# A Fourier input projection on folded operands, moved among the gate units, and an earlier start of the attention scan

## The chip, the cores and the metric

The kernel runs on one core of one Trainium2 chip. The metric is the device time of one execution in microseconds (us). Three runs of the kernel before took 1936.08, 1936.16 and 1936.3 us; the median is 1936.16 us. A profile of one execution on the chip is at hand, with every instruction's start and duration.

## The reference, cut to what matters

One layer of a diffusion backbone on T = 384 positions (128 context, 256 latent) by 2048 channels. The change touches the mixing sub-layer:

```
proj = h @ w_in                     # q 512 | k 512 | v 1024 | g 1024 | lr 32 | fo 1024
o = GLA(q, k, v, decay(lr)); o = rmsnorm(o) * silu(g)            # 4 heads, both directions
fg = fo.reshape(t, 4, 256)
f = fft2(fg, axes=(positions, channels of a group), norm='ortho').real
gates = sigmoid(h @ w_gate + b_gate)
merged = g_a * (o @ w_br_gla) + g_b * (f @ w_br_four)
m = merged @ w_out
```

Context and latent positions are transformed apart (lengths 128 and 256). All adaLN factors are linear maps of a condition, `silu(cond) @ w_ada`, with six blocks of 2048 columns.

## The kernel before, in words

Activations lie transposed, channels on the 128 partitions and the 384 positions along the row; weights come as blocks of 128x1024 f32 (512 KB). The products are f32 in three passes of fp32r: ScalarE (ACT) rounds a weight block to `whi` (L223), VectorE (DVE) forms the rest `wlo = raw - whi` (L224), and TensorE (PE) multiplies `whi` by both parts of the activations and `wlo` by the high one. One "unit" (`proj`) is one block of 128 output columns: two weight blocks ("halves"), each 8 x 3 matmuls of 384 columns.

A list `srcs` fixes the order in which blocks are loaded, and the code consumes them in the same order. `grab` (before each half) takes the next split block and pushes one more: it issues a load into one of two `raw` buffers and splits the block into one of four pairs of `whi`/`wlo` buffers. Three split blocks are ahead of PE at best. PE, ACT, DVE and GpSimd (POOL) run in the order that the code writes; only the DMA queue of SyncE (SP) is ordered by the scheduler.

Beside the products runs side work, handed out by generators: after each half the code calls `next` on them. `ada_rest` computes three of the adaLN blocks on DVE, in six halves of 16 steps (one 512 KB load, two instructions over 128x1024 each, L574), an empty step, a step with 16 small matmuls on the sums (`pr`, L582), and two transposes (`ptm`, L591) at the start of the next half. `paced` throttles it: with `rate` r it advances r steps for each call. It must have ended before the buffer of its sums is reused near the end of `w_out`, so the code empties it after unit 12 of `w_out`.

The stages, with their start in the profile:

- Head (0 us): norm, first adaLN blocks, `h` block by block (`hf`, 16 blocks, kept as `scr`), v and the first two q units (L488 to L529).
- 146 us: the two other q units, the decay factors (`plr`, L812, and the constants `a2`, L814 to L824), four k units; `ada` at rate 1.
- 197 us: 32 gate units (L841), each result stored to DRAM; beside them `ada` at rate 1 and `gla`, the scan of the four heads, in 61 steps.
- 501 us: eight Fourier input units. Two of them make the two half blocks of one group; DVE forms their sum and difference (L952, L953). Then a DFT over channels (`px`, L895, L896) and over positions (`pp`, L881) in plain f32; the result is kept on half of the frequencies only, as `eT` and `dT`.
- 590 us: the mixing stage. Eight units for g ("o", with `gcol`, L982 to L985), 16 Fourier branch blocks ("b", `four`, L998 to L1012, whose weights DVE folds first, L204 and L205) and 16 GLA branch blocks ("a", L1033, L1034) in an order written by hand; `ada` at rate 0.
- 758 us: 16 units of `w_out`, `ada` at rate 0.7. From 893 us: norms and the FFN.

Of the kernel before, what the change touches and what calls it, by code (L numbers as in the profile page):

```python
# [21 lines left out]
P = 128  # L22
# [16 lines left out]
XU = 2  # L39
# [10 lines left out]
HT = HC + HL  # L50
C_CR = C_SEL3 + 96
C_CT = C_CR + 129 + 129 + 128
C_LT = C_CT + 2 * HC
NC = C_LT + 2 * 2 * HL


def _constants():
# [25 lines left out]
    c[:, C_CR : C_CR + 129] = ce  # L83
    c[0, C_CR + 129 : C_CR + 258] = jj[0] % 2
    c[:, C_CR + 258 : C_CR + 386] = cs
    for base, n in ((C_CT, TC), (C_LT, TL)):
        h = n // 2 + 1
        ang = 2 * np.pi * (np.outer(np.arange(n), np.arange(h)) % n) / n
        sc = 1.0 / math.sqrt(n * GD)
        kk = n // P  # L90
        w = kk * h
        for k, m in enumerate((np.cos(ang) * sc, np.sin(ang) * sc)):
            c[:, base + k * w : base + (k + 1) * w] = m.reshape(kk, P, h).transpose(1, 0, 2).reshape(P, w)
# [4 lines left out]
def tile_step(ctx: ExitStack, tc: tile.TileContext, a, o):  # L98
# [48 lines left out]
    for i in range(XU, 8):  # L147
        srcs += two(a["w_in"], i)
    for i in range(32):
        srcs += two(a["w_gate"], i)  # L150
    for i in range(16, 24):
        srcs += two(a["w_in"], i)

    mix_order, n_b = [], 0
    for i in range(8):
        k = (0, 1, 1, 2, 1, 2, 1, 2)[i]
        mix_order += [("o", i)] + [("b", n_b + j) for j in range(k)]
        n_b += k
# [5 lines left out]
    folded = set()  # L164
    for b, i in mix_order:
        if b == "o":
            srcs += two(a["w_in"], 8 + i)
        elif b == "b":
            folded.add(len(srcs))
            srcs.append(a["w_br_four"][i])  # L170
        else:
            srcs.append(a["w_br_gla"][i])
# [17 lines left out]
    def load(raw=None):  # L190
        n, src = next(srcs, (0, None))
        if src is not None:
            if raw is None:
                raw = wp.tile([P, G], F32, tag="raw", name="raw", bufs=2)
            SP.dma_start(raw, src)
            raws.append((raw, n in folded))

    fold_in = []
# [11 lines left out]
    def split(at=None, eng=DVE, hold=False, defer=None):  # L210


        if raws:
            raw, pairs = raws.pop(0)
# [97 lines left out]

    hT = alloc_A()
    psm = ctx.enter_context(tc.tile_pool(name="psm", bufs=3, space=PSUM))
    pss = ctx.enter_context(tc.tile_pool(name="pss", bufs=5, space=PSUM))
    with ExitStack() as s:
# [47 lines left out]
        def load_later():  # L364
# [4 lines left out]
            SP.dma_start(selr, a["consts"][:, C_SELR : C_SELR + 64])  # L369

# [89 lines left out]
        for kb in range(KT):  # L460
# [74 lines left out]
            for sub in lag:  # L535
                sub()
            if kb:
# [8 lines left out]
        push()  # L546
        vr = [actp.tile([P, 3, 1024], F32R, tag=t, name="vr") for t in ("B_hi", "B_lo")]
# [65 lines left out]
    ada = paced(ada_gen, rate)  # L613
    with ExitStack() as s:
# [23 lines left out]
        def gla():  # L638
# [10 lines left out]
            for h in range(NH):  # L649
# [12 lines left out]
                yield  # L662
# [90 lines left out]
                yield  # L753
# [46 lines left out]
            for t in range(3):  # L800
                for h in range(NH):
                    z = on(t, h)
                    DVE.tensor_scalar_mul(z, z, rs[:, t, h : h + 1])
                yield
# [4 lines left out]
        for i in range(XU, 4):  # L809
            proj(psm, hT, keep(qT, i), ada)  # L810
# [14 lines left out]
        for i in range(4):  # L825
            proj(psm, hT, keep(kT, i), ada)

# [10 lines left out]
        for i in range(32):  # L838
            def gate(p, i=i):
                g = pg.tile([P, T], F32, tag="gz", name="gz", bufs=2)  # L840
                ACT.activation(g, p, AF.Identity, bias=bgate[:, i : i + 1])  # L841
                SP.dma_start(gates_d[i], g)

            proj(psm, hT, gate, sd)
# [5 lines left out]
    with ExitStack() as s:  # L850
        pc = s.enter_context(tc.tile_pool(name="pc", bufs=1))
        fold_in.append(pc)
        b0 = C_CR
        pw = 448
        d2 = pc.tile([P, 2 * pw], F32R, name="d2")
        cd = pc.tile([P, NC - b0], F32, name="cd")
        SP.dma_start(cd, a["consts"][:, b0:NC])
        oT = alloc_r("B", "o")


# [5 lines left out]
        nyq = pc.tile([P, 3, P], F32, name="nyq")  # L866
        POOL.memset(nyq, 0.0)


        wn = pc.tile([P, D], F32R, name="wn")  # L870
        done = [0]

        def dft():


            def left(dst, stat, m):

                for lat, base, n in ((0, C_CT - b0, HC), (1, C_LT - b0, HL)):
                    for k in range(1 + lat):
                        c0 = base + (m * (1 + lat) + k) * n  # L880
                        PE.matmul(  # L881
# [1141 lines left out]
```

## Time and profile before

| | |
|---|---|
| median of 3 runs | 1936.16 us (1936.08 to 1936.3) |
| span of the profiled execution, first to last instruction | 1934.3 us |
| PE busy | 1918.5 us (99%) |
| DVE busy | 1641.8 us (85%) |
| ACT busy | 1069.3 us (55%) |
| DMA moved | 429.12 MB, 222 GB/s |

The profiled execution has no time of its own beside its span; the median lies 1.9 us above that span, which is what lies ahead of the first instruction and behind the last one. "PEld" is a weight load of PE, "pmm" the accumulator of a unit. In a row of the chain of waits stand the start, the duration and the work that the time was spent on. In a row of the windows, "x" is a count of instructions. A matmul with two f32 operands shows as two records ("x2").

### The profile page before, as it was taken

To read this page: it belongs to the slowest core of one execution; us is meant where nothing else is said; L and a number is where in the kernel's file an instruction comes from. 1 tells how busy PE (TensorE), PEld (TensorE's weight loads), DVE (VectorE), ACT (ScalarE), POOL (GpSimd) and SP (SyncE) were. 2 spreads that over 40 slices of the span, in tenths; PEclk is the share of its full clock that TensorE was granted. 3 is DMA by queue.
4 is the path that set the end of the run, shared out by engine and by line. 5 is a ranking of instruction groups with operands and counts; after the bars stand their busy time and mean duration, and the time that the engine had idled before them with its cause. 6 is when DMAs were issued, how large, how long until landed. Compare 5 with 4: busy or idle time off the path is not lost.

```text
span 1934.3 us, 27954 instructions
## 1 busy us (share of the span) xinstructions
PE 1918.5 (99%) x10398; PEld 1702.5 (88%) x10398; DVE 1641.8 (85%) x2059; ACT 1069.3 (55%) x1523; POOL 145.2 (8%) x171
## 2 busy tenths in 40 slices
PE   8999999999999999999999999999999999999998
PEld 5779999999999999999988888888888888888886
DVE  5569888879776797977789999999999999988885
ACT  4233454554335655446556666766666666666555
POOL 0000000000000000002100111111111120211001
PEclk9999999999999999999999999999999999999999
DMA  9978676767754687654639696979788797969553
GB/s 389 371 263 269 228 257 219 241 219 259 256 190 145 204 287 246 218 185 154 231 98 280 155 284 151 262 170 244 191 243 207 212 230 192 252 136 253 158 199 128
DMA packets 246152, 429.12 MB, mean 222 GB/s; under 512 B 45308, under 2 KB 149948, under 8 KB 241664
## 3 DMA queue, kind: packets, MB, share of 16 engines
q1 hardware_dynamic: 199072, 386.70, 60.0%
q0 software_dynamic: 18432, 33.56, 11.3%
q10 hardware_dynamic: 28512, 7.08, 2.3%
q8 instruction: 81, 1.33, 0.3%
q14 instruction: 55, 0.45, 0.1%
HBM read 365.68 MB, written 54.53 MB: 217 GB/s over the span
## 4 chain that ended last, share of the span: by engine, by line
PE 97%; DMA 1%; DVE 1%; ACT 0%; issue 0%; SPq 0%; POOL 0%; DVEq 0%; POOLq 0%; ACTq 0%
PE pmm L257 36%; PE pgu L1539 31%; PE pdn L1539 10%; PE pds L1539 7%; PE pv L399 3%; PE pgm L382 1%; PE pf L998 1%; DMA slab<-in_w_ada 1%; PE px L417 1%; PE pmm L1253 1%; PE pf L999 1%; PE bk L1539 1%; PE po L647 1%; PE pr L582 0%; PE dl L647 0%; PE pp L881 0%
## 5 line engine op out<-in xcount | busy, mean ns | idle before, releaser
L257 PE MATMUL pmm<-A_hi,whi 128*128 128x384 f32 x1200 | 404.3, 337 | 0.0
L257 PE MATMUL pmm<-A_hi,wlo 128*128 128x384 f32 x1200 | 401.4, 334 | 0.0
L257 PE MATMUL pmm<-A_lo,whi 128*128 128x384 f32 x1200 | 401.3, 334 | 0.0
L1437 ACT CAST whi<-u 128x1024 fp32r<-128x1024 f32 x200 | 210.1, 1053 | 173.1 <-PE pds L1539 42.6
L223 ACT CAST whi<-raw 128x1024 fp32r<-128x1024 f32 x181 | 189.8, 1051 | 171.3 <-DMA raw<-in_w_gate 62.2
L1448 DVE TENSOR_TENSOR wlo<-u,whi 128x1024 fp32r<-128x1024 f32 x200 | 243.7, 1220 | 34.1 <-ACT whi L1437 32.5
L224 DVE TENSOR_TENSOR wlo<-raw,whi 128x1024 fp32r<-128x1024 f32 x179 | 217.9, 1220 | 52.5 <-ACT whi L223 49.7
L1539 PE MATMUL pgu<-whi,A_hi 128*128 128x512 f32 x640 | 249.9, 390 | 0.0
L1539 PE MATMUL pgu<-whi,A_lo 128*128 128x512 f32 x640 | 249.2, 389 | 0.0
L257 PEld LDWEIGHTS pmm<-A_hi,whi 128*128 128x128 f32 x1200 | 225.3, 188 | 2.9 <-issue 1.8
L257 PEld LDWEIGHTS pmm<-A_lo,whi 128*128 128x128 f32 x1200 | 225.4, 188 | 0.2
L257 PEld LDWEIGHTS pmm<-A_hi,wlo 128*128 128x128 f32 x1200 | 225.3, 188 | 0.0
L574 DVE SCALAR_TENSOR_TENSOR adacc<-adaw,cond,adacc 128x1024 f32<-128x1024 f32 x180 | 222.7, 1278 | 2.8 <-DMA adaw<-in_w_ada 2.5
L1437 ACT CAST whi<-raw 128x1024 fp32r<-128x1024 f32 x157 | 165.0, 1053 | 87.2 <-PE pgu L1539 27.9
L1448 DVE TENSOR_TENSOR wlo<-raw,whi 128x1024 fp32r<-128x1024 f32 x157 | 191.1, 1218 | 12.6 <-ACT whi L1437 12.2
L1539 PE MATMUL pgu<-wlo,A_hi 128*128 128x512 f32 x640 | 185.8, 389 | 0.0
L1539 PEld LDWEIGHTS pgu<-whi,A_hi 128*128 128x128 f32 x640 | 120.1, 188 | 25.9 <-issue 0.8
L1539 PEld LDWEIGHTS pgu<-wlo,A_hi 128*128 128x128 f32 x640 | 120.1, 188 | 25.1
L1539 PEld LDWEIGHTS pgu<-whi,A_lo 128*128 128x128 f32 x640 | 120.1, 188 | 24.7
L1539 PE MATMUL pgu<-whi,S 128*128 128x512 f32 x400 | 116.6, 389 | 0.0
L1672 POOL DMA_DIRECT2D sums_d<-spare x64 | 58.5, 950 | 625.3 <-ACT spare L1668 618.9
L1539 PE MATMUL pdn<-whi,hid_hi 128*128 128x512 f32 x264 | 102.8, 389 | 0.0
(410 smaller groups left out, 3302.3 us busy)
## 6 DMA issues: line engine op xcount, KB each, us to landing
adaw<-in_w_ada SPq DMA_DIRECT2D x96, 512.0 KB, 4.2
raw<-in_w_d SPq DMA_DIRECT2D x70, 512.0 KB, 5.2
slab<-in_w_ada SPq DMA_DIRECT2D x32, 1024.0 KB
raw<-in_w_gate SPq DMA_DIRECT2D x64, 512.0 KB, 4.5
raw<-in_w_g SPq DMA_DIRECT2D x48, 512.0 KB, 3.7
raw<-in_w_u SPq DMA_DIRECT2D x48, 512.0 KB, 5.2
raw<-in_w_in SPq DMA_DIRECT2D x44, 512.0 KB, 4.3
u<-in_w_u SPq DMA_DIRECT2D x40, 512.0 KB, 7.1
```

Source lines behind the costliest of these rows:

```text
L223: ACT.copy(hi, raw)
L224: sub = lambda: eng.tensor_sub(lo, raw, hi.bitcast(F32))
L257: PE.matmul(dst, w[wi][:, k * n + n0 : k * n + n0 + P], x[xi][:, k0 + k, :], start=first and k == 0 and j == 0, stop=last and k == kts - 1 ...
L382: PE.matmul(pgv[q : q + 32, :], spad[:, k, :], slab[k // (KT // 2)][:, k % (KT // 2), :], start=k < 4, stop=k >= KT - 4,)
L399: PE.matmul(pv[2 * t + g], hT[x_][:, kb, t * P : (t + 1) * P], w_[:, g * 512 : (g + 1) * 512], start=kb == 0 and j == 0, stop=kb == KT - 1 ...
L417: PE.matmul(px, w_[:, u * P : (u + 1) * P], hT[x_][:, kb, :], start=j == 0, stop=j == 2)
L574: DVE.scalar_tensor_tensor(acc[:, c, :], w, cond[:, k, c : c + 1], acc[:, c, :], op0=ALU.mult, op1=ALU.add,)
L647: PE.matmul(dst, w[wi], x[xi], start=first and j == 0, stop=last and j == 2)
L1437: ACT.copy(hi, src)
L1448: DVE.tensor_sub(lo, src, hi.bitcast(F32))
L1539: PE.matmul(dst, stat[x_][m], mov(w[w_], m), start=first and w_ == m == x_ == 0, stop=last and w_ == m == 1, skip_group_check=any(more),)
L1672: POOL.dma_start(sums_d[k], u, accum_op=ALU.add)
```

## The change

- In the head, `fold_h` makes sums and differences of mirrored positions of each block of `hf` (DVE), in the place of the spent input, and `keep_h` stores them to DRAM, 1.5 MB in each of two transfers. 194 columns of sums (65 context, 129 latent) and 190 of differences stand for the 384 positions.
- The Fourier input is taken out of the 8 units. The two weight blocks of a group are added and subtracted on DVE (kinds `p0`, `p1`), and the sums are multiplied by the position sums alone, the differences by the position differences alone. The first columns of a pair of blocks (channels 0 and 128 of a group) have no mirror image; their difference on the position sums is added from `bn`, a small product with these columns, which are loaded by themselves (`wnr`, elements of 4 bytes).
- The eight groups' halves are done among the last 8 of the 32 gate units, the folded `h` is read back and split during the two gate units ahead of them, and the DFTs work on the folded positions.
- The k units come first and the scan starts after the first of them, with two steps fewer in each head; the last scaling moves to ACT.
- `ada` runs at rate 1 until gate unit 22, at 0.5 for two units, at 1 to unit 32, at 0.75 in the "o" units of the mixing stage; `w_out` stays at 0.7. Two o units go ahead of the first b.

```diff
+    QK = (4, 5, 6, 7, 2, 3)
+    GF, FO0 = 22, 24
...
     for i in range(32):
         srcs += two(a["w_gate"], i)
+        if i >= FO0:
+            g, kh = divmod(i - FO0, 2)
+            for n in range(2):
+                kinds[len(srcs)] = f"p{n}"
+                srcs.append(a["w_in"][16 + 2 * g + n, kh])
...
-        k = (0, 1, 1, 2, 1, 2, 1, 2)[i]
+        k = (0, 0, 1, 2, 2, 2, 1, 2)[i]
...
+            if kind == "p1":
+                r0 = first_of.pop()
+                ws = fold_in[0].tile([P, G], F32, tag="ws", name="ws")
+                DVE.tensor_add(ws, r0, raw)
+                DVE.tensor_sub(r0, r0, raw)
+                for x in (ws, r0):
+                    hi, lo = (wp.tile([P, G], F32R, tag=t, name=t, bufs=4) for t in ("whi", "wlo"))
+                    split_act(hi, lo, x)
+                    ready.append((hi, lo))
+                return
...
+        def fold_h(kb):
+            f, h = xn(kb), scr[:, kb % 8, :]
+            for n, (e0, e1, c0, c1) in enumerate(((1, 128, TC + 1, T - 1), (HL + 1, HT - 1, 1, TC - 1))):
+                m = e1 - e0
+                up, down = h[:, c0 : c0 + m], h[:, c1 : c1 - m : -1]
+                DVE.tensor_add(f[:, e0:e1], up, down)
+                o0 = HT + n * (HL - 2)
+                DVE.tensor_sub(f[:, o0 : o0 + m], up, down)
...
+        def keep_h(q):
+            SP.dma_start(hf_d[:, 8 * q : 8 * q + 8, :], xnt[q])
...
             for sub in lag:
                 sub()
+            fold_h(kb)
+            if kb == KT - 2:
+                keep_h(0)
...
         push()
+        keep_h(1)
...
-                yield
+                if h == 0:
+                    yield
...
-        for i in range(XU, 4):
-            proj(psm, hT, keep(qT, i), ada)
+        proj(psm, hT, keep(qk, QK[0]), ada)
...
-        for i in range(4):
-            proj(psm, hT, keep(kT, i), ada)
...
+        for i in QK[1:]:
+            proj(psm, hT, keep(qk, i), sd)
+        for i in range(GF):
+            if i < 16:
+                src = a["w_in"][16 + i // 2, i % 2].rearrange("p (k c) -> p k c", c=P)[:, :, 0]
+                SP.dma_start(wnr[:, i // 2, 8 * (i % 2) : 8 * (i % 2) + 8], src)
+            gate_unit(i, sd)
...
+        def parts_of(b):
+            src = fx[:, b % 2]
+            for q in range(4):
+                PE.matmul(
+                    bnp[32 * q : 32 * q + 32, :], wn4[:, 4 * b + q, :], src[:, q, 0:HT], start=b == 0, stop=b == 3,
+                )
+            e = xe[:, 4 * b : 4 * b + 4]
+            split_act(e[:, :, 0], e[:, :, 1], src[:, :, 0:HT])
+            d = xo[b // 2][:, 4 * (b % 2) : 4 * (b % 2) + 4]
+            split_act(d[:, :, 0:HO], d[:, :, HO : 2 * HO], src[:, :, HT:T])
...
+        rate[0] = 0.5
+        for i in range(GF, FO0):
+            gate_unit(i, sd)
...
+                for t, (p0, m) in enumerate(((0, P), (P, HC + 1))):
+                    PE.matmul(px[0:m, t], fe[:, p0 : p0 + m], cd[:, D_CE : D_CE + 129], start=True, stop=False)
+                    PE.matmul(px[0:m, t], bn[:, p0 : p0 + m], cd[:, cb : cb + 129], start=False, stop=True)
...
+        rate[0] = 1.0
+        for i in range(FO0, 32):
+            gate_unit(i, sd)
+            g, kh = divmod(i - FO0, 2)
...
+            for j, n in enumerate((HT, HO)):
+                w, p = grab(), pfo[j]
+                for k in range(8):
+                    x = xo[kh][:, k, :] if j else xe[:, 8 * kh + k].rearrange("p a c -> p (a c)")
+                    c = slice(k * P, (k + 1) * P)
+                    PE.matmul(p, w[0][:, c], x[:, 0 : 2 * n], start=kh == k == 0, stop=False)
+                    PE.matmul(p[:, 0:n], w[1][:, c], x[:, 0:n], start=False, stop=kh == 1 and k == 7)
+                if kh:
+                    f = fs[g][j]
+                    ACT.copy(f, p[:, n : 2 * n])
+                    DVE.tensor_add(f, f, p[:, 0:n])
...
-        rate[0] = 0.0
         mT, late = None, []
         for b, i in mix_order:
             if b == "o":
-                if i == 1:
+                rate[0] = 0.75
+                if i == 2:
                     gate_of()
                 proj(psm, hT, lambda p: gcol(p, i), sd)
...
+                rate[0] = 0.0
```

In `w_out`, not touched by the diff, stands the line that the prediction speaks of:

```
                step(ada)
            if i == KT - 4:
                for _ in ada_gen:
                    pass
```

222 lines of the change are left out of this document (136 added, 86 removed).

## The prediction

> **What bounds the kernel now.** I read the page first, then the windows cut at the stage borders, then the chain of waits and the engines' timelines around the stages that change.
>
> ```profile
> span 1934.3 us, 27954 instructions
> PE 1918.5 (99%) x10398; PEld 1702.5 (88%) x10398; DVE 1641.8 (85%) x2059; ACT 1069.3 (55%) x1523; POOL 145.2 (8%) x171
> ```
>
> PE is idle for 16 us in all. So matmul time that goes comes off the end, as long as no new wait appears on PE. The engine that could make one is DVE. The windows show it by stage (stretch, its length, then busy time of PE, PEld, DVE, ACT, POOL, clock, DMA share, GB/s):
>
> ```profile
> 28.00:100.00 72.00, 71.76 (x561) 52.51 (x560) 44.13 (x98) 19.86 (x37) 0.00 (x0) 1.00 1.00 385
> 146.30:163.00 16.70, 16.70 (x97) 16.63 (x96) 13.73 (x15) 6.25 (x9) 0.00 (x0) 1.00 0.85 287
> 163.00:201.00 38.00, 38.00 (x220) 37.73 (x219) 36.66 (x36) 13.19 (x17) 0.00 (x0) 1.00 0.81 261
> 201.00:488.30 287.30, 287.30 (x1878) 282.76 (x1877) 243.88 (x312) 141.81 (x242) 1.87 (x6) 1.00 0.71 235
> 599.90:676.30 76.40, 76.40 (x481) 76.19 (x480) 58.01 (x109) 51.12 (x73) 0.00 (x0) 1.00 0.59 183
> 676.30:692.30 16.00, 15.36 (x91) 14.75 (x89) 13.36 (x32) 9.23 (x15) 0.00 (x0) 1.00 0.92 319
> 692.30:737.80 45.50, 45.42 (x277) 45.42 (x278) 42.94 (x81) 25.31 (x45) 0.00 (x0) 1.00 0.85 274
> ```
>
> DVE is 96% busy beside the k units, 85% beside scan and gates, 76% in the o/b part of mixing, 94% in its last part. At 692 us it has no lead left; the chain of waits goes through it:
>
> ```profile
> 691.11 1.23 DVE wlo L224
> 692.38 0.36 PE pf L999
> ```
>
> The split ends as PE needs it. Whatever arrives at this point later than now is a wait on PE.
>
> **What PE saves.** The chain gives a Fourier unit, and the f32 DFT products; the PE timeline gives the narrow pair, 388 + 194 columns, that `four` runs already.
>
> ```profile
> 125.84 0.65 PE px L424 x8
> 521.65 0.43 PE px L895 x2
> 522.08 0.22 PE px L896 x2
> 527.81 1.34 PE pp L881 x12
> 602.64 8.35 PE pmm L257 x48
> ```
>
> ```profile
> 601.33 0.36 PE L998 MATMUL pf<-edT,whi 128*128 128x388 f32 x1
> ...
> 602.48 0.36 PE L257 MATMUL pmm<-A_hi,whi 128*128 128x384 f32 x1
> ```
>
> From 601.33 to 602.48 lie four pairs: 0.2875 us each. Eight units of 8.35 us (66.8) become eight times eight sum pairs (2.30 us) and eight difference pairs of 380 + 190 columns (2.25 by columns): 36.4. That saves 30.4 us. The rule of the Trainium skill (TensorE: Matmul & The Clock Gate, Back-to-back issue gap), N/2.4 + 2.5 ns for a matmul alone, would make a pair 0.2475 us, and the saving 5 us larger; the trace does not agree, and the trace is taken.
>
> The DFT of a group is three times 0.65 (0.43 + 0.22) plus 1.34: 3.3 us. New: six products of at most 129 columns (0.22 each, 1.32), two of 194 (1.69 ns a column by the 257-column row, 0.66), one each of 129 and 65 (0.44): 2.42. Four groups save 3.5 us. `bnp` adds four sets of four 32-wide products; L424 is such a set over 384 columns (0.65), so 0.33 by columns, or 0.44 if each pass costs the smallest 0.11 seen: 1.3 to 1.8, take 1.5. PE saves 32.4 us in all.
>
> **What DVE gets.** Start to start, its timeline gives 2.39 us for a step of `ada` and 1.14 for a split; of a "b", 1.92 for the tail and 1.21 for the fold:
>
> ```profile
> 170.99 2.47 DVE L574 SCALAR_TENSOR_TENSOR adacc<-adaw,cond,adacc 128x1024 f32<-128x1024 f32 x2
> 173.38 1.22 DVE L224 TENSOR_TENSOR wlo<-raw,whi 128x1024 fp32r<-128x1024 f32 x1
> 174.52 2.47 DVE L574 SCALAR_TENSOR_TENSOR adacc<-adaw,cond,adacc 128x1024 f32<-128x1024 f32 x2
> ...
> 627.45 0.62 DVE L1003 TENSOR_TENSOR fd<-fd,pf 128x194 f32<-128x194 f32 x2
> ...
> 629.37 0.68 DVE L204 TENSOR_TENSOR ws<-raw 128x512 f32<-128x512 f32 x1
> ...
> 630.58 0.61 DVE L1003 TENSOR_TENSOR fd<-fd,pf 128x194 f32<-128x194 f32 x2
> ```
>
> Gate units 24 to 31. Per unit: four splits 4.6, sum and difference of a pair 2.3, two `ada` steps 4.8, DFT parts 0.7: 12.4 us, beside 8.35 + 4.55 + 1.2 = 14.1 of PE. Covered. In units 22 and 23 DVE has 1.14 + 1.2 and two large splits (1.9) for 4.5 us of PE in each half: covered; the first of the folded blocks and the constants must have come back from DRAM. 0 to 3 us, take 2.
>
> The emptying of `ada` in `w_out`. Six halves take 109 calls. Before: 4 + 8 + 64 + 16 = 92 ahead of mixing, and 17 of the 18 that 26 calls at 0.7 give. After: 2 + 10 + 44 + 2 + 16 + 12 = 86, and 18: 104. Five are left at unit 12, and call 104 falls on the same spot, so three load steps, `pr` and `ptm` come in one lump, and PE, in order, stands at `pr` ahead of unit 13.
>
> ```profile
> 854.35 1.00 PE pr L582 x16
> ...
> 863.88 0.22 PE ptm L591 x2
> 864.10 5.92 PE pmm L257 x34
> ```
>
> ```profile
> 868.85 0.56 DVE L1077 TENSOR_TENSOR qs<-qs,sq 128x384 f32<-128x384 f32 x1 [2.80 <-ACT sq L1066]
> ...
> 871.01 1.22 DVE L224 TENSOR_TENSOR wlo<-raw,whi 128x1024 fp32r<-128x1024 f32 x1
> ```
>
> ```profile
> adaw<-in_w_ada SPq DMA_DIRECT2D x96, 512.0 KB, 4.2
> ```
>
> Before, `pr` came two half units after its last sum. Unit 12 ends 24 matmuls after 864.10, at 868.27; its sums hold DVE to 871.0, 2.7 later. Then steps 13 and 14 to 7.5. Step 15's load needs the buffer of step 13 (two buffers), free at 5.1, and lands at 9.3; its sums end at 11.7; ACT's copy ahead of `ptm` makes it 12 us (10.5 if the load takes 2.5). Nothing covers it.
>
> Mixing. Twelve steps of `ada`, 28.7 us, are added to the eight o units. In the 76.4 us window stand six of these: 9 steps, 21.5 us, on 58.0 busy: 79.5, over PE's time before any wait. DVE's own waits there were
>
> ```profile
> DVE gs L985 <- ACT gs L984: 8.0, 7, 3.5
> DVE wlo L224 <- ACT whi L223: 7.0, 8, 1.4
> DVE o_lo L284 <- ACT o_hi L283: 4.1, 7, 0.6
> ```
>
> `o_lo` follows `gs` through ACT whatever the load (4.1 stays), and so does the split of a fold outside a b (about half of 7.0): some 87 us of DVE in 76.4, 10.7 late. The first two o units carry DFT, the Nyquist weights (fetched only once the Fourier pool is free, with ACT waiting for them) and three steps: 0 to 4 late more. After that the window to 692 leaves 16.0 - 13.4 = 2.6 to catch up, and the next 45.5 - 42.9 = 2.6, too late for the first b's. With 2 us for the first units and 2.6 off it is 10; with loads that start later because their buffers come free later, up to 21; with the ACT waits gone too, 8. Take 14 us.
>
> Scan from the first k unit. Eight halves beside k now hold 36.66 x 8/9.1 = 32 us of DVE. A head takes (243.9 - 61.5 x 3.27)/4 = 10.7 us of DVE (3.27 is a split and 16/18 of an `ada` step); half of it falls ahead of the first attention products, with a wait for ACT's exponentials as in every head (2.9 us, a quarter of this row):
>
> ```profile
> L679 DVE SCALAR_TENSOR_TENSOR la<-z,la 128x512 f32<-128x512 f32 x4 | 2.8, 692 | 11.6 <-ACT la L677 11.6
> ```
>
> 32 + 5.3 + 2.9 = 40 us stand against 8 x 4.17 + 3 = 36.4 of PE: 4 late. The a2 constants must also be ready 8.35 us after `plr`, not 42. `keep_h(1)`, 1.5 MB in front of the next weight blocks, takes 4 to 5 us at the 287 to 385 GB/s of this time (an estimate from the windows) when PE has two blocks in hand: 0 to 3. Take 6 us (2 to 10). Later heads fit: 1.14 + 2.13 + 0.84 (10.7 x 4/51) of DVE in 4.77 of PE.
>
> Hidden. `fold_h` is four short instructions, about 1.0 us, in each of 16 head blocks:
>
> ```profile
> L509 DVE TENSOR_SCALAR mods<-pgm,bsc,norms 128x2 f32<-128x2 f32 x16 | 4.5, 279 | 23.7 <-PE pgm L501 23.7
> L1007 DVE TENSOR_TENSOR y<-fd 128x128 f32<-128x128 f32 x16 | 4.6, 285 | 0.0
> ```
>
> DVE waits 1.5 us per block there for PE; without that cover it would be 16 us. The scaling on ACT (12 short instructions) lies beside gate units.
>
> **Sum.** -32.4 + 12 + 14 + 6 + 2 = +1.6 on the span of 1934.3, and the 1.9 us between span and median: 1938 us. About 0.2% (4 us) can be told from no change; this is inside it.
>
> **Rivals.** DVE's waits vanish (faster). With its queue never empty, DVE stops waiting for ACT in mixing (`gs`: one wait of 3.5) and absorbs the scan: mixing costs 79.5 - 76.4 = 3, the scan 2, the lump 12: -32.4 + 17 = -15, 1921 us. For it: PE never waited in the k window with DVE at 96%. Against: the lead was already nil at 692.
>
> The 4-byte loads (slower). `wnr` is 16 transfers of 1024 elements of 4 bytes, 64 for each DMA engine, on the queue that also brings the weights.
>
> ```profile
> q1 hardware_dynamic: 199072, 386.70, 60.0%
> q10 hardware_dynamic: 28512, 7.08, 2.3%
> ```
>
> A packet costs 93 ns on q1 (0.6 x 16 x 1934 / 199072) and 25 ns on q10, where packets hold 250 bytes: 1.6 to 6 us for each transfer, 26 to 95 in all. Spread over 16 gate units (150 us) the DMA share goes from 0.71 to 0.88 at the low price, to 1.3 at the high one. It decides from 45 ns a packet on, or sooner if SP issues them in one burst beside the k units (share 0.81): then 15 us on top of the forecast, 1953 us. The Trainium skill says that a non-contiguous last dimension becomes one descriptor per element and should be made contiguous (DMA: Bandwidth & Descriptors, Rules for kernel authors); no run so far shows the price.
>
> **How the numbers follow.** The forecast has 0.52 (its own range 1929 to 1946: 0.04 faster, 0.24 same, 0.24 slower), DVE's waits gone 0.36 (0.32 faster, 0.04 same), the small loads 0.12 (slower). So 0.36 faster, 0.28 same, 0.36 slower. The range reaches to both rivals' middles: 1916 to 1952.
>
> **What would show it.** PE busy falls by about 32 us. Right: `pr` with a PE wait of 10 to 12 us ahead of unit 13 of `w_out`; waits for `wlo` of L224 at half the b's, 8 to 21 us in all; a wait at the first `z` or `at`. Wrong: no wait at `pr`; mixing without waits for `wlo` (first rival); waits of ACT for `raw` in the gate units with a DMA share near 1 (second); a sum pair that is not 0.29 us.

## The result and the profile after

The changed kernel takes 1980.09 us (median of 4 runs, 1978.28 to 1984.04) against 1936.23 us (1936.08 to 1937.08) on the same chip: a ratio of 1.0227, 95% interval 1.0213 to 1.0242. The change costs 44 us. The forecast was 1938, and 1980 lies outside its range. The medians below leave out three single executions of 2130 to 8555 us, one each of f_px, m_yield and n_scale, which stand far from all the others of the same kernels.

The top of the page after, with the clock row of the part in 40 slices (each about 49 us):

```profile
span 1976.7 us, 27848 instructions
PE 1912.3 (97%) x10284; PEld 1682.4 (85%) x10284; DVE 1673.7 (85%) x2136; ACT 1078.3 (55%) x1566; POOL 145.4 (7%) x172
...
PEclk9999999999999999998999999999999999999999
```

PE's busy time fell by 6 us where 32 were forecast, while the span grew by 42. Three things make up most of the difference. The saving itself was some 4 us smaller, as shown further below. A matmul of 384 columns has a record of 0.33 us though the next one starts 0.17 us behind it, so the last one ahead of each wait adds a little busy time. And there is something that the page before had nowhere: a slice whose clock is an 8. The waits of PE, by the tile waited for (total us, times, longest):

```profile
PE pf L1113 <- DVE wlo L256: 10.3, 9, 1.5
PE pr L634 <- DVE adacc L626: 10.1, 1, 10.1
PE pmm L289 <- DVE wlo L256: 6.0, 6, 2.5
PE px L995 <- ACT nyq L998: 5.8, 4, 4.2
PE at L797 <- DVE ki L774: 5.1, 2, 4.6
...
PE ptm L643 <- ACT adacc L639: 2.9, 2, 2.4
PE kr L717 <- ACT qk L870: 2.5, 1, 2.5
...
PE px L1001 <- ACT xc L1002: 2.2, 4, 0.6
```

Of these, the waits at `pr` and `pf` had been forecast, and so had a wait at the first `at`. The waits at `px`, at `ptm` and at `kr` had not. In the windows, cut where the same work starts in both kernels (first k and q unit; first transpose `pt` of an o unit; last `pf` of a b; first `pst` of the norms), columns as in the prediction, before:

```profile
146.10:589.10 443.00, 443.00 (x2798) 436.68 (x2797) 371.32 (x443) 198.68 (x339) 4.15 (x9) 1.00 0.72 237
589.10:737.80 148.70, 147.98 (x916) 147.12 (x915) 118.83 (x226) 89.33 (x139) 0.00 (x0) 1.00 0.67 216
737.80:893.10 155.30, 155.30 (x908) 154.43 (x907) 122.42 (x154) 73.19 (x117) 0.00 (x0) 1.00 0.62 204
```

and after, with the first stretch cut once more at the first `cr` of the scan and the first Fourier product:

```profile
146.10:202.90 56.80, 48.26 (x289) 46.59 (x289) 41.60 (x51) 24.96 (x36) 1.03 (x3) 0.96 0.80 219
202.90:461.40 258.50, 255.67 (x1658) 249.10 (x1655) 214.96 (x273) 129.60 (x232) 2.64 (x8) 0.99 0.71 236
461.40:589.60 128.20, 120.11 (x731) 115.67 (x730) 94.45 (x94) 48.85 (x81) 0.95 (x1) 0.97 0.67 213
589.60:764.80 175.20, 156.71 (x911) 150.46 (x909) 151.26 (x254) 90.94 (x141) 0.95 (x1) 0.98 0.68 223
764.80:935.30 170.50, 159.77 (x925) 156.83 (x925) 131.40 (x165) 73.18 (x118) 0.00 (x0) 0.96 0.60 197
```

So the first three stretches take 443.5 us where the work alone was to make 443.0 into about 411, mixing takes 175.2 in the place of 148.7, and the w_out stretch 170.5 in the place of 155.3. From 935 us on the two kernels run alike. The sum of the three is +42.2 us. In none of these five stretches is the clock 1.00.

Where the clock falls, windows cut at the borders of the intervals show 0.50. Seven intervals, each 3.4 us or a multiple of it, begin during or shortly behind waits of PE of 2.2 us and more; two of them, and the sum of all seven:

```profile
489.10:495.90 6.80, 6.34 (x22) 5.71 (x21) 3.99 (x4) 2.11 (x5) 0.00 (x0) 0.50 0.73 233
...
898.70:912.30 13.60, 6.31 (x30) 4.55 (x31) 7.22 (x10) 0.37 (x1) 0.00 (x0) 0.50 0.30 101
sum 37.50, PE 29.21 PEld 26.71 DVE 26.35 ACT 10.72 POOL 0.61; mean PE 4.17 PEld 3.82 DVE 3.76 ACT 1.53 POOL 0.09
```

In 37.5 us at half clock PE was busy for 29.2; if that work takes half as long at full clock, some 14.6 us were lost there, on top of the waits themselves (a_wout and p_lump below bear the half out). The Trainium skill (TensorE: Matmul & The Clock Gate, Part 1: The HAM clock gate) says that the clock is halved after an idle window of about 3.4 us, in windows that run freely. The trace agrees with the length and the half, and shows it after shorter waits too (2.4 us at `ptm`).

The theory that follows: separate waits of PE, each made by where one step stands in the queue of DVE or ACT, or behind one transfer, and each with its share of half clock. The rivals: that DVE, with more work and a shorter span, is full, so that a wait taken away in one place comes back in another; and that the added transfers do it. All experiments but one start from the changed kernel; gains are against its 1980.1. The kernel before, run beside each of them, took 1936.2 to 1936.5 us.

### The profile page after: what moved, and what is told of

Its sections match the earlier page's. It is cut to its first block, busy times and chain, and to the rows that moved or that the text cites. A ratio compares the mean times of both kernels' runs of the same rounds, so it can differ in the third digit from the quotient of the medians.

```text
span 1976.7 us, 27848 instructions
## 1 busy us (share of the span) xinstructions
PE 1912.3 (97%) x10284; PEld 1682.4 (85%) x10284; DVE 1673.7 (85%) x2136; ACT 1078.3 (55%) x1566; POOL 145.4 (7%) x172
## 3 DMA queue, kind: packets, MB, share of 16 engines
q0 software_dynamic: 18432, 33.56, 11.2%
## 4 chain that ended last, share of the span: by engine, by line
PE 82%; DVE 9%; DMA 4%; ACT 3%; issue 2%; SPq 0%; POOL 0%; DVEq 0%; ACTq 0%; POOLq 0%
PE pgu L1664 30%; PE pmm L289 23%; PE pdn L1664 10%; PE pds L1664 7%; DVE adacc L626 3%; PE pv L447 3%; DMA raw<-in_w_in 2%; DVE wlo L256 2%; PE pgm L430 1%; PE pfo L1038 1%; PE px L465 1%; PE pmm L1378 1%; ACT whi L255 1%; DMA adaw<-in_w_ada 1%; PE bk L1664 1%
## 5 line engine op out<-in xcount | busy, mean ns | idle before, releaser
L289 PE MATMUL pmm<-A_hi,wlo 128*128 128x384 f32 x1072 | 362.9, 339 | 5.4 <-DVE wlo L256 5.3
L289 PE MATMUL pmm<-A_hi,whi 128*128 128x384 f32 x1072 | 366.1, 341 | 0.0
L289 PE MATMUL pmm<-A_lo,whi 128*128 128x384 f32 x1072 | 362.5, 338 | 0.0
L256 DVE TENSOR_TENSOR wlo<-raw,whi 128x1024 fp32r<-128x1024 f32 x163 | 198.7, 1222 | 69.9 <-ACT whi L255 69.3
L255 ACT CAST whi<-raw 128x1024 fp32r<-128x1024 f32 x165 | 172.7, 1050 | 152.3 <-DMA raw<-in_w_gate 52.4
L1562 ACT CAST whi<-raw 128x1024 fp32r<-128x1024 f32 x157 | 165.0, 1052 | 92.3 <-PE pgu L1664 25.8
L289 PEld LDWEIGHTS pmm<-A_hi,wlo 128*128 128x128 f32 x1072 | 204.1, 190 | 7.6 <-DVE wlo L256 7.3
L289 PEld LDWEIGHTS pmm<-A_hi,whi 128*128 128x128 f32 x1072 | 204.6, 191 | 4.3 <-issue 2.7
L289 PEld LDWEIGHTS pmm<-A_lo,whi 128*128 128x128 f32 x1072 | 204.3, 191 | 0.2
L1573 DVE TENSOR_TENSOR wlo<-raw,whi 128x1024 fp32r<-128x1024 f32 x157 | 191.6, 1221 | 12.4 <-ACT whi L1562 12.1
```

What stands on the lines that cost most here:

```text
L255: ACT.copy(hi, raw)
L256: sub = lambda: eng.tensor_sub(lo, raw, hi.bitcast(F32))
L289: PE.matmul(dst, w[wi][:, k * n + n0 : k * n + n0 + P], x[xi][:, k0 + k, :], start=first and k == 0 and j == 0, stop=last and k == kts - 1 ...
L1562: ACT.copy(hi, src)
L1573: DVE.tensor_sub(lo, src, hi.bitcast(F32))
```

## The experiments

**a_wout: the lump in w_out.**

```
-        rate[0] = 0.7
+        rate[0] = 0.95
```

> The changed kernel with one number different: ada runs at rate 0.95 in w_out in the place of 0.7, so that its last five steps are handed out before unit 13 and nothing is left to empty. First theory (stalls, and the clock that falls after them): the changed kernel's trace has PE waiting 10.1 us at pr, 0.5 more at ptm, and then the granted clock at 0.5 from 898.7 to 912.3 us; 6.9 us of that has PE at work at half speed, which is another 3.5 us. All of it goes: 14 us less, 1966 us (1963 to 1968), with no interval at half clock in w_out. Rival: only the lump's own wait goes and the half clock was there for another cause: 10 us less, 1970. Second rival: DVE has no room for 2.39 x 0.95 = 2.3 us of ada beside 1.14 us of split in 4.17 us, and waits for wlo appear in w_out: over 1972.

Measured: 1966.2 us, 13.9 less, and no half clock from 820 us to the norms:

```profile
820.00:922.50 102.50, 102.50 (x603) 101.64 (x602) 91.50 (x109) 47.12 (x76) 0.00 (x0) 1.00 0.65 215
```

The first theory holds, with its half clock; DVE had the room.

**p_lump: the same lump in the kernel before.**

```
-        rate[0] = 0.7
+        rate[0] = 0.47
```

> The kernel before the change with one number different: ada at rate 0.47 in w_out in the place of 0.7, so that the same five steps are left to empty after unit 12 as in the changed kernel. First theory (a wait of 10 us at pr, and half clock after it, cost 14 us, whatever stands ahead): 1950 us (1948 to 1952), a wait of 10 to 10.5 us at pr and three or four intervals of 3.4 us at half clock, in a kernel that has none. Rival (the half clock in the changed kernel had another cause, such as the shorter Fourier matmuls): the wait alone, 1946 to 1947, clock 1.0 throughout.

Measured: 1949.8 us (ratio 1.0066, 1.0053 to 1.0079), 13.4 more than before. The wait and the interval behind it, from its waits and its windows:

```profile
PE pr L582 <- DVE adacc L574: 10.2, 1, 10.2
...
870.10:883.80 13.70, 5.79 (x28) 4.03 (x29) 7.78 (x10) 0.37 (x1) 0.00 (x0) 0.50 0.25 80
```

10.2 at `pr`, 0.5 at `ptm` and half of 5.8 make 13.6. In a kernel whose only other waits of over 1 us stand at its very start and end, this one wait brings the half clock with it. So an interval needs nothing of the change but the wait.

**b_mix0: mixing without ada.**

```
-                rate[0] = 0.75
+                rate[0] = 0.0
...
-        rate[0] = 0.5      # units 22 and 23
+        rate[0] = 1.0
...
-        rate[0] = 0.7      # w_out
+        rate[0] = 1.35
```

> The changed kernel without ada in the o units of the mixing stage (rate 0 in the place of 0.75); its 12 steps go elsewhere: rate 1 in gate units 22 and 23, and 1.35 in w_out, which also leaves nothing to empty after unit 12. First theory (DVE's load in mixing makes the waits): mixing, from the first o unit to the first unit that stands alone after the b's, falls from 173.3 us back to 147 to 150, waits for wlo at the b's fall from about 16 us to under 3, and w_out loses its 15 us lump but may gain a few us since DVE has 1.14 + 1.35 x 2.39 = 4.4 us of work for each 4.17 us of PE: 1943 us in all (1936 to 1950). Rival (the order of the units, two o units ahead of the first b, with the folds and the late DFT, makes the waits): mixing stays above 163 us, and the total is 1955 to 1965.

Measured: 1970.9 us, which neither gave, but the stretch answers:

```profile
589.80:741.50 151.70, 149.32 (x910) 147.19 (x908) 121.17 (x227) 89.19 (x140) 0.95 (x1) 1.00 0.66 214
```

Mixing falls from 175.2 to 151.7, within 3 us of the kernel before, so the order of the o units is not the cause; the 12 steps of ada are. The rest of the expectation fails: w_out takes 183.6 us in the place of 155.3. With 33 steps there PE waits 10.0 us at `pr` and 9.1 for splits, again with half clock. Most of what was taken from mixing and from the lump came back.

**f_px: another order in the DFT.** The products first, the copies behind them:

```
                 for t, (p0, m) in enumerate(ev):
                     PE.matmul(px[0:m, t], ...)
                     PE.matmul(px[0:m, t], ...)
+                px2 = pss.tile([P, 2, P], F32, tag="side", name="px")
+                for t, (p0, m) in enumerate(od):
+                    PE.matmul(px2[0:m, t], ...)
+                for t, (p0, m) in enumerate(ev):
                     ACT.copy(xc[0][0:m, t], ...)
                     ACT.copy(nyq[0:m, t, ...], ...)
```

> The changed kernel with the DFT over channels in another order: all six small products of a group first, into two accumulators, and ACT's six copies behind them, so that PE no longer waits for ACT's copy of one part before it writes the next part of the same accumulator. In the changed kernel PE waits 5.8 us for nyq at L995 (4.2 of it in the first group, followed by 6.8 us at half clock) and 2.2 at L1001. First theory (the wait comes from that order, and the half clock from the wait): px waits under 1 us in all, no half clock near 489 us, 8 to 10 us less: 1971 us (1969 to 1973). Rival (ACT itself is late, since its queue stands at a split that waits for a weight block, and the products over positions, which need the copies, wait in their place): 3 us less at most, 1977 or more, with waits at L980.

Measured: 1968.3 us, 11.8 less. The Fourier stretch falls from 128.2 to 116.9 us with the clock at 1.00:

```profile
460.10:577.00 116.90, 116.23 (x733) 113.04 (x732) 94.29 (x94) 47.77 (x81) 0.95 (x1) 1.00 0.72 232
```

What the wait was made of is seen in ACT's timeline of the changed kernel (start, duration, work, in brackets the idle time before it and what ended it) and PE's row at the same moment:

```profile
485.91 1.05 ACT L315 CAST whi<-ws 128x1024 fp32r<-128x1024 f32 x1 [5.84 <-DVE ws L239]
487.17 1.04 ACT L315 CAST whi<-rp 128x1024 fp32r<-128x1024 f32 x1 [0.21 <-DVE rp L240]
488.12 0.36 ACT L997 COPY xc<-px 128x256 f32<-128x256 f32 x1
488.38 0.17 ACT L998 COPY nyq<-px 128x3 f32<-128x3 f32 x1
...
488.60 0.44 PE L995 MATMUL px<-cd,fs 128*66 128x129 f32 x2 [4.20 <-ACT nyq L998]
```

The accumulator is ready at 484.4, but ACT works in order and stands at a split whose block comes from a DVE sum, which begins at 484.6 when its load has landed and ends at 485.8. The copies, half a microsecond of work, wait 3.7 us behind it, and PE waits for the copies before it may write the next part of the same accumulator. The first theory holds; with the order turned the copies lie beside the next half unit.

**n_scale: the last scaling back on DVE.**

```
-                    ACT.mul(z, z, rs[:, t, h : h + 1])
+                    DVE.tensor_scalar_mul(z, z, rs[:, t, h : h + 1])
```

> The changed kernel with the last scaling of the attention output on DVE, where it was before the change. In the changed kernel's trace the 12 instructions hold ACT from 422.4 to 427.3 us, ACT's copy of pr stands behind them, and PE waits 2.4 us at ptm, followed by 3.4 us at half clock. First theory: that wait and that half clock go, 4 us less: 1976 us (1974 to 1977). Rival (DVE, with 3.4 us more in the same place, makes the next split late, and PE waits for wlo in its stead): within 1.5 us of the changed kernel.

Measured: 1973.8 us, 6.3 less, of which 3.7 in the stretch where it stands (from the first `cr` to the first Fourier product 254.8 us in the place of 258.5). The wait of 2.4 us at `ptm` is gone, and the half clock behind it; the other 2.6 us of the gain lie elsewhere and were not taken apart. In the changed kernel ACT's queue was

```profile
422.42 4.90 ACT L867 ACTIVATE qk<-qk,rs 128x256 f32<-128x256 f32 x12 [0.30 <-DVE rs L863]
427.23 0.35 ACT L639 COPY adacc<-pr 128x256 f32<-128x256 f32 x1
...
427.63 0.69 PE L643 MATMUL ptm<-ident,adacc 128*128 128x128 f32 x2 [2.38 <-ACT adacc L639]
```

**c_qk0, d_nownr, e_nokeep, r_early: the scan's early start.** Three suspects, each left out alone, then together. c_qk0 and r_early hand the steps of ada that are left out here to gate units 22 and 23 and to w_out (rate 1.35); e_nokeep and r_early read the first half of the stored input twice, and d_nownr and r_early leave out the first-column correction.

```
+        rate[0] = 0.0                      # c_qk0, r_early
         for i in QK[1:]:
             proj(psm, hT, keep(qk, i), sd)
+        rate[0] = 1.0
...
-                SP.dma_start(wnr[...], src)  # d_nownr, r_early
...
-        keep_h(1)                          # e_nokeep, r_early
```

> The changed kernel without ada beside the last five k and q units (rate 0 there), which takes 10 steps, 24 us, from DVE between 155 and 204 us; they go to gate units 22 and 23 (rate 1) and to w_out (rate 1.35). The first cr product stands at 202.9 us in the changed kernel. First theory (DVE's load beside these units makes the waits at z and at): cr comes 7 to 9 us earlier, at 194 to 196 us, and the 4.7 us wait at `at` is gone. Rival (the transfers of this stretch and ACT's exponentials make them): cr at 200 us or later. In all the time says less, since w_out cannot take the steps: it was 28 us longer than before the change when it had 33 of them, and has 31 here: 1983 to 1990 by the first theory, 1990 to 1995 by the rival.

> The changed kernel without the 16 loads of 4-byte elements; wnr is filled with zeros, so the first-column correction of the Fourier input is left out of the result while all its products still run. In the trace of the changed kernel the 16 loads are issued from 165.5 to 186.6 us in four bursts, SP is held 16 us by them, and 16 thousand packets of 9 ns keep the 16 DMA engines busy for 9.2 us; but the weight blocks behind them were still waiting for DVE to free a buffer, except for 0.6 us at 170.4. First theory (DVE and the scan make the waits in the k units): 0 to 3 us less, 1977 to 1981. Rival (the loads delay the weight blocks beside the k units): the waits at kr, z and at lose 8 us or more: under 1972.

> The changed kernel without the second store of the folded input (1.5 MB, issued at 141.3 us ahead of two weight blocks); the second half of the folded input is read from the first half's place, so that half of the Fourier input is computed from the other half's channels. In the changed kernel's trace the split of the third block in hand starts at 151.45 us, before the change the same split started at 147.1, and PE then waits 2.6 us at kr, because the copy of the first k unit stands behind the splits in ACT's queue. First theory (this store is what PE waits for at kr, and the half clock from 161.4 follows from that wait): 3 to 6 us less, 1974 to 1977, with no half clock at 161. Rival (the a2 constants and DVE's steps of ada decide): within 1.5 us of the changed kernel, and kr or z still waits.

> Three things left out at once between 146 and 204 us: the second store of the folded input (half of the Fourier input is then computed from the other half's channels), the 4-byte loads (no first-column correction), and ada beside the last five k and q units (its steps moved as in c_qk0). In the changed kernel the first cr product stands at 202.9 us; the same matmuls without any wait and at full clock would bring it to about 192.5. Apart, leaving out each brought it to 198.1, 198.1 and 197.2. First theory (these three make the whole loss of the scan's early start, each by its own wait): 192.5 to 195. Rival (they share one chain of waits, whose rest, ACT's exponentials and its place in the queue, is reached by any of them): 196 or later.

Measured: 1972.7, 1973.4, 1974.0 and (two executions) 1967.9 us. The first `cr` stands at 197.2, 198.1, 198.1 and 192.1. Alone, c_qk0 and d_nownr lie between what their two theories gave, and e_nokeep at the edge of its first one (no wait at `kr`, no half clock at 161 us); the total of c_qk0 came out 10 us better than either said, about half of it since w_out took its 31 steps in 178.6 us, where b_mix0 had 183.6 with 33. To read them, one must know how far this place moves by itself: in six traces in which nothing up to there was changed (the changed kernel, a_wout, b_mix0, f_px, j_pool, n_scale) it stands at 199.6 to 202.9, 201.0 on the mean. Against that mean the three bring back 3.8, 2.9 and 2.9 us, 9.6 in all, and all three together 8.9. They add up, as the first theory of r_early said, and what is left is a stretch without a wait:

```profile
146.10:192.10 46.00, 46.00 (x293) 45.32 (x293) 28.78 (x41) 25.68 (x38) 0.00 (x0) 1.00 0.59 191
```

So the loss here has three causes of similar size: DVE's ada steps, the second store of the folded input, and the 4-byte loads. Each size rests on one trace, in a place that moves by 3.3 us by itself, so which is the largest is not shown. For the loads there are two traces more: in i_comb and q_comb3 below, where they are held back and nothing else is changed up to there, the first `cr` stands at 198.4 and 198.0. The totals of d_nownr and e_nokeep fell by more, 6.7 and 6.1 us; part of that is an interval of half clock behind the second o unit, which these two traces lack, and the rest was not taken apart.

The store is seen in ACT's splits. Before the change the first two splits behind the head stood at

```profile
147.10 1.05 ACT L223 CAST whi<-raw 128x1024 fp32r<-128x1024 f32 x1 [0.20 <-DMA raw<-in_w_in]
151.34 1.05 ACT L223 CAST whi<-raw 128x1024 fp32r<-128x1024 f32 x1 [3.20 <-DMA raw<-in_w_in]
```

and after it at

```profile
151.45 1.05 ACT L255 CAST whi<-raw 128x1024 fp32r<-128x1024 f32 x1 [4.54 <-DMA raw<-in_w_in]
156.50 1.05 ACT L255 CAST whi<-raw 128x1024 fp32r<-128x1024 f32 x1 [3.99 <-DMA raw<-in_w_in]
```

In e_nokeep they stand at 147.67 and 151.80, near where they stood before. The 4-byte loads are seen on SP's queue and in the DMA view of 182.0 to 187.3 us:

```profile
165.53 4.78 SPq L902 DMA_DIRECT2D wnr<-in_w_in x4
...
177.47 9.77 SPq L902 DMA_DIRECT2D wnr<-in_w_in x9
```

```profile
q1 hardware_dynamic: 5756, 0.02, 60.8%
```

SP issued them between 165.5 and 187.2 us, ahead of the gate units to which the code writes them one by one. Each issue held SP for 1.1 to 1.2 us in these two bursts, and for 0.55 to 0.67 in the other three issues. A packet took 0.608 x 5.3 us x 16 / 5756 = 9 ns.

**m_yield: two more pauses in the first head.**

```
             for h in range(NH):
+                if h == 0:
+                    yield
...
+                if h == 0:
+                    yield
                 ats = []
```

> The changed kernel with two more pauses in the first head of the scan: its first product comes one half unit later, and one more half unit lies between the second set of exponentials and `at`. First theory (PE waits at kr, z and at since ACT and DVE come to the scan's steps late in their own order, and 4.2 us of products put between cover it): the waits at kr, z and at, 9.4 us in the changed kernel, fall under 3, and the half clock at 161 and 202 us goes: 9 to 12 us less, 1969 us (1967 to 1972). Rival (the stretch is bound by DVE's whole load, 24 us of ada and 16 of scan, so that the waits come at wlo in their place): 4 us less or nothing, 1976 or more.

The change had taken one pause out of the first head and two out of each of the others. Measured: 1980.9 us, no gain, as the rival had it. The waits at `kr`, z and `at` fell to 0.4 us, but 4.0 us of waits for a split of the scan and for `wlo` came ahead of `at`, and behind the scan's later end `bnp` waited 4.6 us.

**j_pool: the Fourier weight sums on GpSimd.**

```
-                DVE.tensor_add(ws, r0, raw)
-                DVE.tensor_sub(r0, r0, raw)
+                POOL.tensor_add(ws, r0, raw)
+                POOL.tensor_sub(r0, r0, raw)
```

> The changed kernel with the sums and differences of the Fourier weight blocks on GpSimd in the place of DVE, 16 instructions over 128x1024 elements, 1.24 us each on DVE. First theory (DVE's queue is what makes the blocks, and with them ACT, late in the Fourier part): with 18 us less for DVE there, the px waits fall from 8 to under 3 us and the total by 3 to 6: 1975. Rival (GpSimd is the slower place: more than 3 us for one of these instructions, 6 for a pair, ahead of ACT's split): waits at the Fourier products, 1985 or more.

Measured: 1991.5 us, 11.4 more. The rival, though at a lower price than it named:

```profile
L240 POOL TENSOR_TENSOR rp<-rp,raw 128x1024 f32<-128x1024 f32 x8 | 22.2, 2776 | 0.6
L239 POOL TENSOR_TENSOR ws<-rp,raw 128x1024 f32<-128x1024 f32 x8 | 19.2, 2395 | 108.9 <-DMA raw<-in_w_in 73.3 <-PE bnp L940 24.9 <-DVE edT L316 10.7
```

A pair takes 5.2 us against 2.5 on DVE, and it lies on the way from load to ACT's split: the `px` waits grew from 8.0 us to 13.4. Less load on DVE did not help: in this trace PE waits for the delay of the block, not for DVE's sum of work.

**i_comb: the repairs together.** The edits of f_px, rate 1 in units 22 and 23, and

```
+                ACT.copy(wnr[...], bgate[:, 0:8])
                 SP.dma_start(wnr[...], src)
...
-                rate[0] = 0.75
+                rate[0] = 0.2      # o units
-                rate[0] = 0.0
+                rate[0] = 0.4      # a blocks
...
-        rate[0] = 0.7
+        rate[0] = 1.0              # w_out
```

> The changed kernel with what the runs so far point to, together: the order of the DFT as in f_px; each 4-byte load tied to its gate unit by a small ACT copy into its place, so that the 16 loads no longer go out in bursts beside the k units; ada at rate 1 in gate units 22 and 23, at 0.2 in the o units, 0.4 beside the a blocks and 1.0 in w_out, so that nothing is left to empty. First theory (separate stalls, each with its share of half clock, that add): 14 us less for the lump, 19 for mixing, 9 for the DFT, 4 for the loads, 2 back for a fuller DVE in w_out: 1936 us (1928 to 1946). Rival (DVE has no room left anywhere between 146 and 893 us, so that what leaves one stage comes back as a wait in another): 1950 or more.

Measured: 1944.5 us (ratio 1.0047, 1.0031 to 1.0063): 36 less than the changed kernel, within the range of the first theory, but still over the kernel before. Mixing still had 10.1 us of `pf` waits, with only six load steps of ada in it in the place of twelve.

**l_comb2: ada out of mixing, the scan eased.** As i_comb, with no ada in mixing but 0.5 beside the last five a blocks, 1.05 and 1.2 in the gate units, the pauses of m_yield and the scaling of n_scale.

> As i_comb, with the steps of ada moved once more and the scan's start eased: no ada in the o units and beside the a blocks until the b's are over (0.5 beside the last five), 1.05 in the gate units, 1.2 in the last eight of them, 1.0 in w_out; in the first head of the scan one half unit more ahead of its first product and one more ahead of `at`; the last scaling of the attention output on DVE again. The trace of i_comb has left: 14 us of waits in mixing (pf waits of 10.1), 3.6 at `at`, 2.3 at z with 6.8 us at half clock behind `at`, 2.4 at ptm with 3.4 us at half clock. First theory (each of these is a wait made by where a step stands in a queue): 10 us less in mixing, 7 at the scan's start, 4 at ptm: 1924 us (1918 to 1932), faster than before the change. Rival (DVE is full, and what is taken out of mixing comes back at the Fourier products or in w_out): 1938 or more.

Measured: 1944.4 us (ratio 1.0040, 1.0026 to 1.0054): on the rival's side in time. The trace is of the slowest of nine executions (1952.4 us). Mixing did fall in it, to 151.4 us from the first `pt` to the last `pf`, and what it gained was lost ahead of it: the first Fourier product stands at 472.4 us, 14.5 later than in i_comb, behind the pauses, a lump at the scan's end and two steps of ada in one half unit.

**q_comb3 and q_comb4: the best place found for each step.** q_comb3 is i_comb with the scaling of n_scale, without ada in mixing but beside the last five a blocks, 1.04 in w_out and four steps of ada in a place of their own:

```
             if kh:
                 done[0] = g + 1
+                next(ada, None)
```

q_comb4 has the store of the folded input in three parts besides:

```
-            if kb == KT - 2:
-                keep_h(0)
+            if kb == 10:
+                keep_h(((0, 8),))
+            if kb == KT - 2:
+                keep_h(((8, 13),))
...
-        keep_h(1)
+        keep_h(((13, 16),))
```

> The best part of each run so far put together: from i_comb the order of the DFT, the 4-byte loads tied to their gate units, rate 1 in gate units 22 and 23 and the scan as in the changed kernel; from n_scale the last scaling on DVE; from l_comb2 no ada in the o units nor beside the a blocks before the last five (0.5 there); one step of ada more after the Fourier products of units 25, 27, 29 and 31, where DVE has time; 1.04 in w_out. Theory (the stages are separate, and each keeps what it had in its own run): 1944.5 less 12 for mixing (i_comb took 163.0 us from the first transpose of the o units to the last pf, l_comb2 151.4), less 4 at ptm, plus 1 to 2 for the extra steps: 1930 us (1924 to 1936), faster than before the change by 0.1 to 0.6%. Rival (the steps of ada have no place where DVE takes them without a wait of PE): 1938 or more.

> As q_comb3, with the folded input stored in three parts of 8, 5 and 3 blocks, after blocks 10 and 14 of the head and at its end, in the place of 8 and 8 after block 14 and at the end; 0.56 MB in the place of 1.5 stand ahead of the weight blocks at 141 us. Theory (the store's size in front of the weight blocks is what delays them): 3 to 5 us less than q_comb3. Rival (the DMA engines are full in the head, their share 0.88 to 1.0, and an earlier store delays the head's own loads by as much): no less than q_comb3, with the head's end after 146.3 us.

Measured: 1928.6 us (ratio 0.9960, 0.9947 to 0.9972) and 1925.7 us (0.9948, 0.9935 to 0.9962). Both beat the changed kernel, and the kernel before by 0.4 and 0.5%. The theory gave 1930 for the first; the second lies 2.9 lower, just under the 3 to 5 expected, and the two intervals overlap, so the store's part rests on the stretch (first `cr` at 196.9 in the place of 198.0) and on e_nokeep. The windows of q_comb4, cut as those of the changed kernel:

```profile
146.10:196.90 50.80, 46.62 (x291) 45.54 (x291) 41.69 (x52) 25.25 (x37) 1.03 (x3) 0.99 0.68 230
196.90:451.10 254.20, 253.88 (x1658) 247.54 (x1656) 222.75 (x289) 126.36 (x236) 2.65 (x8) 0.99 0.76 245
451.10:568.20 117.10, 116.48 (x733) 112.90 (x732) 102.20 (x102) 46.98 (x81) 0.96 (x1) 1.00 0.75 239
568.20:719.20 151.00, 149.37 (x910) 147.15 (x909) 122.30 (x228) 89.60 (x140) 0.95 (x1) 1.00 0.69 224
719.20:882.40 163.20, 159.45 (x926) 156.44 (x926) 145.39 (x181) 73.55 (x119) 0.00 (x0) 0.99 0.67 227
```

DVE does the same work as in the changed kernel (634.3 us over these windows, 633.7 there) in 53 us less. So it was not full, and the rival that it was falls; what differs is the order of the work. The last stretch is still 7.9 us longer than before the change: some 1.5 of that is one more set of `pr` and `ptm` matmuls, which stood in an earlier stretch before, 3.7 is waits of PE, and 1.7 is the loss in one interval of half clock.

## Why the prediction was wrong

Two terms that were taken as covered were not, the half clock behind waits was put at nothing, and the term for mixing was too small. The terms, one by one:

**What PE saves** was nearly right. The Fourier products take 37.4 us (36.4 forecast) and `bnp` 1.9 (1.5). The DFT saves less: in f_px and q_comb4, where it does not wait, its `px` and `pp` products take 11.6 to 11.7 us against 12.8 before the change, a saving of 1.1 and not 3.5. In all about 28.5 us, not 32.4.

**The lump** was right as a mechanism, down to the 10.1 us at `pr` (10.5 to 12 forecast), with `pr` in the place and for the reason given. Its cost was 13.9, because the half clock behind it was missing.

**Mixing** was right as a mechanism: waits for `wlo` at the b's, made by the 12 steps of ada. The size was 26.5 us and not 14 (8 to 21). b_mix0 gives 23.5 of it to ada; the other 3.0 are there without ada too. The listed waits come to 18.5 us there (10.3 and 2.2 at `pf`, 6.0 at `pmm`), within the forecast bounds, and two intervals of half clock take another 3.5 (half of 3.5 and of 3.4 us with PE busy throughout). The term assumed that DVE would arrive late once, by the excess of its work, and then keep that lag; the chain shows that it is late anew in each unit, since an ada step stands in front of a split there, at 633 us as at 628:

```profile
632.10 0.52 ACT o_hi L315
...
632.65 0.04 DVE o_lo L316
632.69 0.44 issue
633.13 2.48 DVE adacc L626 x2
635.60 1.14 DVE wlo L256
```

**The scan** was forecast at 6 (2 to 10) and cost about 9, 10.8 in the profiled run. DVE's excess was put at 4 and measured at 3.8. The store, put at 0 to 3, cost 2.9. The 4-byte loads were kept for a rival and cost 2.9; that rival's condition, a burst beside the k and q units, is near to what happened (four groups within 22 us), while its price per packet was wrong (9 ns, below both ends of 25 to 93), so that it added a few us and not 15.

**The steps that failed outright** are two covers and one omission. "Covered", for gate units 24 to 31, compared sums of work, 12.4 us of DVE and 14.1 of PE; by sums it was covered, but the DFT's order of product, copy, product made PE wait for ACT, and ACT stood behind a split: 11.3 us. "The scaling on ACT (12 short instructions) lies beside gate units": it does, in front of a copy for which PE waits; about 4 us (3.7 by the stretch of n_scale, 4.1 by the wait and half of its interval). And every wait was counted at its own length, with nothing for the clock, while the losses at half clock come to some 14.6 us; they lie inside the shares that follow, not beside them.

The shares: from +1.6 to +42.2, mixing is 12.5, the DFT's order 11.3, the smaller saving on PE 3.9, the scaling some 2 beyond the 2 allowed for units 22 and 23, the scan 3 to 5 and the w_out stretch 3.2. These sum to 36 to 38; the other 3 to 5 us no run took apart.

Of the first rival, that DVE's waits in mixing vanish, a part was seen: its waits for `gs` fell there from 9.8 to 4.6 us. Those of its splits for `whi` stayed (11.2 before, 10.8 after), and PE waited 18.5 us all the same.

## What to carry to other kernels

Read cover by order, not by sums. For each instruction that PE waits for, look at what stands ahead of it on its in-order engine, and whether that may itself wait for a load; and price a wait of over 2 us of a busy PE at its length plus up to half of the next 3.4 us or more. When work moves between stages, its new place must be free in each half unit: here nearly the same work on DVE came with 44 us lost in the first order, and with 11 gained once the steps, the DFT, the scaling, the loads and the store had other places.

## What the runs showed of the hardware

- The clock falls by half in steps of 3.4 us after waits of PE, and the same wait does not always bring it. The wait of 2.4 to 2.5 us in the second o unit was followed by an interval in the changed kernel, a_wout, f_px, c_qk0 and m_yield, and by none in d_nownr, e_nokeep, n_scale and r_early. Single waits of 1.5 us mostly had none. From 146 us on, all waits of over 3.3 us had one, of 3.4 to 13.7 us; behind the wait of 4.1 us at the first `px` it was 3.4 us in n_scale and 10.2 in a_wout. This may be why four runs of the changed kernel spread over 5.8 us and four of the kernel before over 1.0, which no run tests.
- Loads of single 4-byte elements cost 9 ns a packet on a DMA engine, 0.57 us for each 1024 over 16 engines, but 0.55 to 1.2 us of SP, where a 512 KB weight load holds it for 0.33.
- GpSimd takes 2.4 to 2.8 us for an f32 sum of 128x1024 in this place, DVE 1.24.
